# Encoder layer, the hand-over from the convolutions to the tail: two gate jobs make their own first products, net outputs rotate over seven rooms, five units of fillers stand in one fixed order

## The chip, the core and the metric

One core of a Trainium2 chip runs the whole layer as one program. The metric is the device time of one launch in microseconds (us), the median of several runs. The engines that matter here are TensorE (PE, matrix products, with PEld for its weight loads), VectorE (DVE), ScalarE (ACT), GpSimd (POOL) and SyncE, whose queue (SP) issues most DMA transfers. Each engine works through its own list of instructions in order; semaphores hold an instruction back until what it needs is there.

## The reference, cut to what matters

Two batches of 1024 rows by 1024 channels go through the same layer (`y_prompt` and `y_sample`, here b = 0 and b = 1):

```python
p = rmsnorm(x, g_pre) @ w_in
fv, fg, hv, hg, mg = split(p)          # widths 1024, 1024, 3072, 1024, 2048
fz  = fft over sequence and over 4 channel groups of fv, real part
y_f = (fz * silu(fg)) @ w_fourier_out
v, x1, x2 = split(short_conv(hv, w_short))
z = v
for n, gate in enumerate((x1, x2)):
    z = gate * long_conv(z, kf[:, n], hyena_d[n])      # by FFT of length 2L
y_h = (z * silu(hg)) @ w_hyena_out
g_f, g_h = split(sigmoid(mg + b_merge))
out = (g_f * y_f + g_h * y_h) @ w_out
y = x + rmsnorm(out, g_post)
```

## The kernel before, in words

Everything is float32. A product is made of three passes of TensorE: each operand is cut into a rounded high part and a rest (`split`: a cast on ACT, a subtraction on DVE or POOL), and high x high, high x low and low x high are added up in PSUM. Twelve matmuls of 128x512 (four blocks of the inner dimension, three passes) are the unit of work in what follows; `times` issues twelve.

Three phases follow one another: `phase_fourier`, `phase_main` (gates and convolutions) and `phase_tail`.

**The end of the main phase.** `branches` walks over 32 steps, 16 for each batch; a step is one long convolution of 128 channels (`conv_front`, `conv_back`). The last four steps also take units of *fillers* from the list `FIRST`, one, one, two and two; the units left over run after the last step. A unit (`spill_first`, L1062 to L1104) holds two gate jobs. A job is named (section, c): sections 5 and 6 are the two merge gates, 0 and 4 the SiLU gates of the two branches, and c is a group of 128 channels. For each job of a unit it makes twelve matmuls over the first half of the inner dimension (q = 0), then twelve over the second (q = 1), both into its half of one PSUM tile `pin`. Behind the q = 0 matmuls ACT copies the half sum into a tile `m` (L1091), and SP stores it in DRAM as `d_p` (L1092): the tail needs that half sum once more. Each batch of twelve matmuls wants a loaded weight `wr` (L1080, two rooms), cut into `wh` and `wl` (three rooms of each).

A unit called with `wide` true has more room: two more rooms for weights (`wx`), one tile of its own for both `m`, another for `fz`; and its first matmuls are put behind the last ones of the unit before it (`self.filler`), so that wide units run in one order, batch by batch. Units called with `wide` false are placed by the scheduler as it likes. Before, only the units of the last step and those behind it are wide: four of eight.

**The tail, its gates.** `phase_tail` makes the second half of batch 1's gates. Its 16 jobs (list `gates`) cover two groups of channels and two halves of the rows each, by Winograd's form of Strassen's scheme: seven products of twelve matmuls in place of eight. `PH` names them for the nets: 11, 12, s2, s1, s4, s3, 22. The first two products of each job were made in the main phase; `opened` (L1458) loads `m` = `d_p`, and ACT copies it into PSUM, where the next products are added. Each job so has five products left: s2 x T2, s4 of the job before x B22, s3 x T3, 22 of the job before x T4, s1 x T1. The left operands come from `prepare`, a generator that is advanced by hand between the products: load `wraw` (1 MB), then sums and splits s2, s3, s1, s4, 22. The right operands T1 to T4 lie in four `rooms` of 1 MB, loaded from `d_t` (`load_t`) and split in place (`round_t`). `gate_out` evacuates a result to a `gt` tile and stores it in `d_g`; in sections 0 and 4 it also loads `fz`, applies SiLU and multiplies.

**The tail, its nets.** Then come 4 x 28 products (`product(s)`, s = 0 to 111) for the two output projections of each branch and batch. `load_w` and `weight` bring and split their weights, `block` their right operands, and `step` places that work at fixed points between the products. Sixteen of each 28 products end in `net_out` (L1571): DVE subtracts or adds into a `gt` tile (three rooms), multiplies by the gate `g`, and the result goes to `d_m`: by SP in nets 0 and 2, and by POOL with an accumulating DMA (L1582) in nets 1 and 3. A room is free again once its transfer has landed. Eight `rows` of the last projection follow; `opening` prepares the first one of them while net 3 still runs, in the tiles s1h, s1l and sum among others.

The tile framework gives every engine its order by simulating the program; `tc.issue_after(i)` puts instructions of the same engine behind instruction `i`. A dependency between tiles counts the whole tile: the q = 0 matmuls of a unit's second job wait for the copy of the first job's half sum.

Of the kernel before, what the change touches and what calls it, by code (L numbers as in the profile page):

```python
# [16 lines left out]
P = 128  # L17
# [144 lines left out]
class K:  # L162
# [897 lines left out]
    def spill_first(self, jobs, ws, wide):  # L1060


        nc, a, wp = self.nc, self.a, self.wp
        ps = self.psum("mm", 2, "pin", L)
        at = lambda i: ps[:, 512 * i:512 * i + 512]
        last = self.filler if wide else None
        room = self.xp.tile([P, L], F32, tag="x13", name="m", bufs=1) if wide else None
        fz = self.xp.tile([P, L], F32, tag="x12", name="fz", bufs=1) if wide else None
        for q in range(2):
            for i, (sec, c) in enumerate(jobs):  # L1070
                k = self.taken % 5
                self.taken += wide
                if wide and k < 2:
                    t = self.xp.tile([P, 2, 512], F32R, tag=f"x1{k}", name="wx", bufs=1)
                    h, l = [t[:, j].rearrange("p (a b) -> p a b", a=4) for j in range(2)]
                else:
                    h, l = [wp.tile([P, 4, P], F32R, tag=t, name=t, bufs=3) for t in ("wh", "wl")]
                hf, lf = [t.rearrange("p a b -> p (a b)") for t in (h, l)]
                r = wp.tile([P, 512], F32, tag="w", name="wr", bufs=2)
                self.filled = nc.sync.dma_start(r, a["w_in"][sec, c][:, 512 * q:512 * q + 512])  # L1080
                self.split(hf, lf, r, "pool", "act")
                self.pooled = self.left
                with self.tc.issue_after(last.ins) if last else ExitStack():
                    for kk in range(4):
                        x = self.X[4 * q + kk][0]
                        for j, (w, d) in enumerate(((h, x[0]), (h, x[1]), (l, x[0]))):
                            done = self.mm(at(i), w[:, kk], d, q + kk + j == 0, kk + j == 5, True)
                last = done
                if q == 0:
                    m = room[:, 512 * i:512 * i + 512] if wide else wp.tile([P, 512], F32, tag="gt", name="m", bufs=3)  # L1090
                    nc.scalar.copy(m, at(i))  # L1091
                    nc.sync.dma_start(self.d_p[sec, c], m)  # L1092
        for i, (sec, c) in enumerate(jobs):
            t = wp.tile([P, 512], F32, tag="gt", name="gt", bufs=3)
            if sec in (0, 4):
                f = fz[:, 512 * i:512 * i + 512]
                nc.sync.dma_start(f, (self.d_sh if sec else self.d_fz)[1][c][:, 0:512])
                nc.scalar.activation(t, at(i), AF.Silu)
                self.mul("dve", t, t, f)
            else:  # L1100
                nc.scalar.copy(t, at(i))
            nc.sync.dma_start(self.d_g[1][sec][c][:, 0:512], t)
        self.filler = last
# [147 lines left out]
    def branches(self, nb, nct, ws, mi):  # L1251
# [49 lines left out]
        for i, (b, n, c) in enumerate(steps):  # L1301
            nxt = None
            if i + 1 < len(steps):
                nxt = front(i + 1)
                gates(i + 1)
                if i + 2 < len(steps) and steps[i + 2][0] != steps[i + 1][0]:
                    self.load_x(steps[i + 2][0])
            y = self.conv_back(n, c, B, ws)
            close(i + 1)
            B = nxt  # L1310
            for _ in range({4: 1, 3: 1, 2: 2, 1: 2}.get(len(steps) - i, 0)):
                self.spill_first(units.pop(0), ws, i + 1 == len(steps))
            z = self.gate(n, c, y, X.pop(i))
            if self.due:
                mark = mi.tile([P, 1], F32R, tag="mark", name="mark", bufs=1)
                with tc.issue_after(nc.gpsimd.tensor_copy(mark, z[:, 0:1]).ins):
                    self.due.pop(0)()
            if n == 0:
                Z[c] = z
                continue  # L1320
            nc.sync.dma_start(self.d_sh[b][c], z)
            if b == 0 and NF <= c:
                self.spill_gate(0, 0, c, ws)
# [17 lines left out]
        self.stt("dve", s[:, 1], s[:, 0], -1.0, r[:, 3], MUL, SUB)  # L1341
        self.add("dve", s[:, 3], s[:, 1], r[:, 2])

    FIRST = [((s, c), (s, c + 2)) for s in (5, 6) for c in (0, 4)] + [((0, c), (4, c)) for c in range(0, 8, 2)]

    def block_sums(self, r, u, k, rows):

# [36 lines left out]
    def phase_tail(self):  # L1384
# [2 lines left out]

        tc, nc, a = self.tc, self.nc, self.a
        wp, xp = self.wp, self.xp
        gates = [(s, c) for c in range(0, 8, 2) for s in (0, 4, 5, 6)]  # L1390
        rows = [(u, t) for u in range(4) for t in (0, 2)]
        nets = [("f", 0), ("h", 0), ("f", 1), ("h", 1)]
        flat = lambda t: t.rearrange("p a b -> p (a b)")
# [1 line left out]
        with ExitStack() as es:  # L1395
# [7 lines left out]
            def prepare(nm, s, c):  # L1403
# [16 lines left out]
                    A[n] = h, l  # L1420
                if opening:
                    parts("11", wp, ("w", "w"), r[:, 0], 2)
                elif nm == "o":
                    parts("11", wp, ("wh", "wl"), r[:, 0], 3)
                    parts("12", wp, ("wh", "wl"), r[:, 1], 3)
# [33 lines left out]
            def opened(job):  # L1459
                m = wp.tile([P, 512], F32, tag="wh", name="m1", bufs=3)  # L1460
                nc.sync.dma_start(m, self.d_p[job])
                p = self.psum("X", 2, "pg")
                if job in gates[:2]:
                    x = self.X[4][1][0]
                    self.mm(p, x[:, 0:P], x, True, True)
                nc.scalar.copy(p, m)
                return p

            def first(A, Y):
                pa, pb = self.psum("mm", 4, "pg"), self.psum("X", 2, "pg")  # L1470
                self.times(pa, A["11"], Y["B11"], True)
                m1 = kept(pa)
                self.times(pb, A["12"], Y["B21"], True)
                return pa, pb, m1
# [96 lines left out]
            def net_out(s, p, q, op2):  # L1571
                nm, b = nets[s // 28]
                c, m, o = out_of(s)
                t = wp.tile([P, 512], F32, tag="gt", name="gt", bufs=3)
                if q is not None:
                    self.tt("dve", t, p, q, op2)
                self.mul("dve", t, p if q is None else t, G[s])
                dst = self.d_m[2 * b + m][:, c]
                if nm == "f":
                    nc.sync.dma_start(dst, t)  # L1580
                else:
                    nc.gpsimd.dma_start(dst, t, accum_op=ADD)  # L1582
# [166 lines left out]
            rooms = [gs.tile([P, 2, 4, 512], F32R, tag=f"t{q}", name=f"room{q}", bufs=1) for q in range(4)]  # L1749
            act, dve, sp = self.rounded.ins.engine, self.left.ins.engine, self.filled.ins.engine  # L1750
            behind = lambda: tc.issue_after(newest(sp))
            prep = prepare("g", *gates[0])
            with tc.issue_after(self.filled.ins):
                next(prep)
            for j, q in order[:2]:
                with behind():
                    load_t(rooms[q], 0, int(j[1]) - 1)
            with behind():
                pa = opened(gates[0])
            j, q = order[2]  # L1760
            with behind():
                load_t(rooms[q], 0, int(j[1]) - 1)
            next(prep)
            Y = {"B22": [self.X[4 + k][1] for k in range(4)]}
            for j, q in order[:2]:
                for k in range(2):
                    round_t(rooms[q], k)
            pairs = lambda z: [(t[:, 0], t[:, 1]) for t in z]
            quad = lambda t: [(t[:, 0, k], t[:, 1, k]) for k in range(4)]
            for j, q in order:  # L1770
# [15 lines left out]
            A = list(next(prep) for _ in range(2))[-1]  # L1786
            for k in range(2):
                round_t(rooms[order[2][1]], k)
            past = None
            for i, job in enumerate(gates):  # L1790
                to = i + 1 - len(gates)
                more = prepare("g", *gates[i + 1]) if to else None
                ahead_of = (lambda: next(more)) if to else (lambda: None)

                def mark(n):
                    t = n - 5 + 5 * to
                    if t >= -6:
                        step(t)
                with ExitStack() if i else behind():
                    ahead_of()  # L1800
                if i == 0:
                    with behind():
                        load_t(rooms[order[3][1]], 0, 3)
                self.times(pa, A["s2"], Y["T2"], False)
                u = wp.tile([P, 512], F32, tag="wl", name="u", bufs=3)
                nc.scalar.copy(u, pa)
# [25 lines left out]
                B = ahead_of()  # L1832
                past = job, A, pa, pc, u
                if to:
                    A, pa, prep = B, opened(gates[i + 1]), more
                    if 2 <= i < 6:
                        r = [cell(xp, f"x1{2 * (i % 2) + j}", f"ws{j}") for j in range(2)]
                        with tc.issue_after(self.fetched.ins):
                            pinned(self.block_sums, [r[q // 2][:, q % 2] for q in range(4)], 1, i - 2,
                                   [a["w_out"][(i - 2 + 4 * j) * P:(i - 1 + 4 * j) * P] for j in range(2)])  # L1840
# [136 lines left out]
```

## Time and profile before

| what | us |
|---|---|
| median of the runs shown (2368.45 to 2373.16) | 2372.25 |
| the profiled execution, its own time | 2370.79 |
| its span in the trace | 2369.0 |
| PE busy | 2325.3 (98%) |
| DVE busy | 1985.3 (84%) |
| ACT busy | 1126.1 (48%) |
| POOL busy | 417.8 (18%) |
| mean granted TensorE clock | 0.995 |

The page counts a matmul from its start to its modelled end, and consecutive matmuls overlap: a busy PE is one without gaps, not one at its peak. In the traces below a start time is in us from the start of the span, then comes the duration; a bracket at the end of a timeline row says how long the engine had been idle and what ended that.

### The profile page before, as it was taken

How to read it: one execution, taken by the hardware profiler on the slowest of the kernel's cores; microseconds unless marked ns; L12 is line 12 of the kernel's file. 1: busy time of each engine (PE TensorE's matmuls, PEld its weight loads, DVE VectorE, ACT ScalarE, POOL GpSimd, SP SyncE). 2: the span in 40 equal slices, each digit the busy share in tenths (PEclk: the TensorE clock that was granted, in tenths of full speed). 3: DMA queues.
4: the chain of work that ended last, by engine and by line, in shares of the span. 5: the costliest groups of instructions: out<-in, count | busy, mean ns of one | idle time of the engine just before them, and what ended most of it. 6: DMA issues, size and time to landing. Idle time of an engine off the chain costs nothing.

```text
span 2369.0 us, 36468 instructions
## 1 busy us (share of the span) xinstructions
PE 2325.3 (98%) x12834; PEld 2019.9 (85%) x12834; DVE 1985.3 (84%) x3485; ACT 1126.1 (48%) x2111; POOL 417.8 (18%) x405
## 2 busy tenths in 40 slices
PE   8999999999999999999999999998999999999998
PEld 7998888888888888888888888886878888788787
DVE  8875788888889999999999989996766677786887
ACT  7645667666643333333322223333434465466443
POOL 1002212322432343330000001123000000101211
PEclk9999999999999999999999999999999999999999
DMA  8636855455766666667556555567875788989654
GB/s 281 231 106 227 274 188 173 154 176 175 231 224 211 197 218 205 213 179 249 172 176 177 173 163 163 185 198 249 285 257 188 254 296 265 245 281 272 169 160 142
DMA packets 255425, 496.50 MB, mean 210 GB/s; under 512 B 25606, under 2 KB 83304, under 8 KB 254922
## 3 DMA queue, kind: packets, MB, share of 16 engines
q1 hardware_dynamic: 231229, 419.03, 54.3%
q0 software_dynamic: 23792, 75.11, 11.3%
q8 instruction: 101, 1.65, 0.3%
q14 instruction: 82, 0.67, 0.1%
q10 hardware_dynamic: 221, 0.04, 0.0%
HBM read 339.41 MB, written 181.93 MB: 220 GB/s over the span
## 4 chain that ended last, share of the span: by engine, by line
PE 46%; issue 6%; DMA 4%; DVE 3%; POOL 1%; ACT 1%; SPq 0%; DVEq 0%; POOLq 0%; ACTq 0%
PE pin L195 17%; PE pg L195 12%; PE pn L195 6%; PE pT L195 5%; PE pX L195 5%; DMA room<-d_t 1%; PE tph L1115 1%; DMA d_m<-gt 1%; DMA ws<-in_w_out 1%; DMA wraw<-in_w_in 1%; DMA oB<-d_wo 0%; POOL d_m L1582 0%; DVE gt L182 0%; DMA wr<-in_w_in 0%; DVE ws L182 0%
## 5 line engine op out<-in xcount | busy, mean ns | idle before, releaser
L195 PE MATMUL pin<-x,wh 128*128 128x512 f32 x2760 | 872.3, 392 | 7.7 <-ACT m L1091 7.7
L195 PEld LDWEIGHTS pin<-x,wh 128*128 128x128 f32 x2760 | 513.4, 189 | 105.8 <-ACT m L1091 8.7
L195 PE MATMUL pin<-x,wl 128*128 128x512 f32 x1380 | 540.8, 392 | 0.0
L182 POOL TENSOR_TENSOR wl<-wr,wh 128x512 fp32r<-128x512 f32 x137 | 235.7, 1721 | 701.1 <-ACT wh L172 665.6
L195 PEld LDWEIGHTS pin<-x,wl 128*128 128x128 f32 x1380 | 260.1, 188 | 49.1
L195 PE MATMUL pn<-room,wh 128*128 128x512 f32 x864 | 268.2, 392 | 1.9 <-DVE gt L182 1.9
L195 PEld LDWEIGHTS pn<-room,wh 128*128 128x128 f32 x864 | 163.2, 189 | 37.3 <-DVE gt L182 2.8
L195 PE MATMUL pn<-room,wl 128*128 128x512 f32 x432 | 169.5, 392 | 4.2 <-DVE wl L182 4.2
L182 DVE TENSOR_TENSOR t<-pX,k 128x1024 f32<-128x1024 f32 x128 | 156.2, 1220 | 8.9 <-DMA k<-d_k 5.1
L195 PE MATMUL pX<-bh,cfwd 128*128 128x256 f32 x768 | 161.7, 289 | 0.6 <-DVE t L182 0.6
L172 ACT CAST wh<-wr 128x512 fp32r<-128x512 f32 x137 | 84.7, 618 | 130.1 <-PE pin L195 70.8
L195 PE MATMUL pT<-cinv,yh 128*128 128x256 f32 x768 | 145.3, 284 | 0.5 <-DVE T0s L182 0.5
L172 ACT CAST bh<-b 128x512 fp32r<-128x512 f32 x144 | 88.6, 619 | 94.2 <-DVE b L182 65.7
L195 PEld LDWEIGHTS pX<-bh,cfwd 128*128 128x128 f32 x768 | 126.4, 190 | 3.7 <-DVE t L182 1.5
L195 PEld LDWEIGHTS pT<-cinv,yh 128*128 128x128 f32 x768 | 122.6, 191 | 5.9 <-issue 0.6
L1582 POOL DMA_DIRECT2D d_m<-gt x32 | 27.3, 884 | 536.5 <-DVE gt L182 535.4
L172 ACT CAST yh<-y 128x512 fp32r<-128x512 f32 x96 | 59.4, 619 | 126.9 <-DVE y L182 126.8
L195 PE MATMUL pT<-cinv,yl 128*128 128x256 f32 x384 | 109.2, 284 | 0.5 <-DVE yl L182 0.4
L195 PE MATMUL pX<-bl,cfwd 128*128 128x256 f32 x384 | 109.3, 285 | 0.0
L182 DVE TENSOR_TENSOR bl<-b,bh 128x512 fp32r<-128x512 f32 x144 | 103.0, 719 | 5.0 <-ACT bh L172 4.9
L195 PEld LDWEIGHTS pn<-room,wl 128*128 128x128 f32 x432 | 81.8, 189 | 21.8 <-DVE wl L182 4.6
L182 DVE TENSOR_TENSOR y<-t 128x512 f32<-128x512 f32 x128 | 93.7, 732 | 3.0 <-PE pT L195 2.5
(383 smaller groups left out, 5124.5 us busy)
## 6 DMA issues: line engine op xcount, KB each, us to landing
k<-d_k SPq DMA_DIRECT2D x128, 512.0 KB, 4.3
wr<-in_w_in SPq DMA_DIRECT2D x144, 256.0 KB, 3.6
d_g<-gt SPq DMA_DIRECT2D x124, 256.0 KB, 2.9
wl<-d_s SPq DMA_DIRECT2D x56, 512.0 KB, 5.4
d_k<-kt SPq DMA_DIRECT2D x128, 128.0 KB, 2.3
d_k<-kt SPq DMA_DIRECT2D x64, 256.0 KB, 2.7
wraw<-in_w_in SPq DMA_DIRECT2D x32, 512.0 KB, 4.8
g<-d_g SPq DMA_DIRECT2D x64, 256.0 KB, 5.2
```

Source lines behind the costliest of these rows:

```text
L172: self.rounded = nc.scalar.copy(h, src)
L182: return e.tensor_tensor(out, a, b, op=op)
L195: return self.nc.tensor.matmul(out, lhsT, rhs, start=start, stop=stop, skip_group_check=shared)
L1115: nc.tensor.transpose(tp[:, q * P:(q + 1) * P], eo[:, e, q], self.ident)
L1582: nc.gpsimd.dma_start(dst, t, accum_op=ADD)
```

## The change

1. Jobs (5, 0) and (6, 0) (`OPEN`) leave the fillers: seven units of two jobs are left of eight, 14 half sums of 16. At the head of the tail, `prepare` also splits their operands 11 and 12, and `first` makes their two products (24 matmuls a job) into PSUM tiles of their own; the ACT casts for it are put behind the last copy of a half sum (`self.held`). They go in front of `gates`, whose order of sections becomes 5, 6, 0, 4 in place of 0, 4, 5, 6. Their first result leaves through `gate_out` right there.
2. The loads at the head of the tail are in this order, each behind the one before: `wraw` of the first job, `wraw` of the second, T2, T3, T1, T4. Before, it was `wraw` of the first, T2, T3, the half sum of the first, T1, then `wraw` of the second, T4.
3. The two matmuls in `opened` that only filled PSUM tiles of the first two jobs (into `pg`, from `x` alone) go.
4. The units of the last two steps are wide (`len(steps) - i < 3`), with those behind them five of seven.
5. Net outputs with s < 84 rotate over seven rooms (three `gt`, then the tiles u, s1h, s1l and sum, which the gates have left), those of net 3 over four (three `gt` and u).

```diff
@@ -1088,7 +1088,7 @@
                 last = done
                 if q == 0:
                     m = room[:, 512 * i:512 * i + 512] if wide else wp.tile([P, 512], F32, tag="gt", name="m", bufs=3)
-                    nc.scalar.copy(m, at(i))
+                    self.held = nc.scalar.copy(m, at(i))
                     nc.sync.dma_start(self.d_p[sec, c], m)
         for i, (sec, c) in enumerate(jobs):
             t = wp.tile([P, 512], F32, tag="gt", name="gt", bufs=3)
@@ -1309,7 +1309,7 @@
             close(i + 1)
             B = nxt
             for _ in range({4: 1, 3: 1, 2: 2, 1: 2}.get(len(steps) - i, 0)):
-                self.spill_first(units.pop(0), ws, i + 1 == len(steps))
+                self.spill_first(units.pop(0), ws, len(steps) - i < 3)
             z = self.gate(n, c, y, X.pop(i))
             if self.due:
                 mark = mi.tile([P, 1], F32R, tag="mark", name="mark", bufs=1)
@@ -1341,7 +1341,8 @@
         self.stt("dve", s[:, 1], s[:, 0], -1.0, r[:, 3], MUL, SUB)
         self.add("dve", s[:, 3], s[:, 1], r[:, 2])
 
-    FIRST = [((s, c), (s, c + 2)) for s in (5, 6) for c in (0, 4)] + [((0, c), (4, c)) for c in range(0, 8, 2)]
+    OPEN = [(5, 0), (6, 0)]
+    FIRST = [((5, 2), (5, 4)), ((6, 2), (6, 4)), ((5, 6), (6, 6))] + [((0, c), (4, c)) for c in range(0, 8, 2)]
 
     def block_sums(self, r, u, k, rows):
 
@@ -1387,7 +1388,7 @@
 
         tc, nc, a = self.tc, self.nc, self.a
         wp, xp = self.wp, self.xp
-        gates = [(s, c) for c in range(0, 8, 2) for s in (0, 4, 5, 6)]
+        gates = [(s, c) for c in range(0, 8, 2) for s in (5, 6, 0, 4)]
         rows = [(u, t) for u in range(4) for t in (0, 2)]
         nets = [("f", 0), ("h", 0), ("f", 1), ("h", 1)]
         flat = lambda t: t.rearrange("p a b -> p (a b)")
@@ -1420,6 +1421,15 @@
                     A[n] = h, l
                 if opening:
                     parts("11", wp, ("w", "w"), r[:, 0], 2)
+                elif nm == "g" and (s, c) in self.OPEN:
+                    for j in range(2):
+                        if (s, c) == self.OPEN[0]:
+                            t = cell(gw, f"st{j}", "wa", F32R)
+                            self.split(t[:, 0], t[:, 1], r[:, j], "dve", "act")
+                            A[("11", "12")[j]] = tri(t[:, 0]), tri(t[:, 1])
+                        else:
+                            parts(("11", "12")[j], wp, ("wh", "wl"), r[:, j], 3)
+                    yield A
                 elif nm == "o":
                     parts("11", wp, ("wh", "wl"), r[:, 0], 3)
                     parts("12", wp, ("wh", "wl"), r[:, 1], 3)
@@ -1460,14 +1470,11 @@
                 m = wp.tile([P, 512], F32, tag="wh", name="m1", bufs=3)
                 nc.sync.dma_start(m, self.d_p[job])
                 p = self.psum("X", 2, "pg")
-                if job in gates[:2]:
-                    x = self.X[4][1][0]
-                    self.mm(p, x[:, 0:P], x, True, True)
                 nc.scalar.copy(p, m)
                 return p
 
-            def first(A, Y):
-                pa, pb = self.psum("mm", 4, "pg"), self.psum("X", 2, "pg")
+            def first(A, Y, *where):
+                pa, pb = [self.psum(*w, "pg") for w in (where or (("mm", 4), ("X", 2)))]
                 self.times(pa, A["11"], Y["B11"], True)
                 m1 = kept(pa)
                 self.times(pb, A["12"], Y["B21"], True)
@@ -1571,7 +1578,11 @@
             def net_out(s, p, q, op2):
                 nm, b = nets[s // 28]
                 c, m, o = out_of(s)
-                t = wp.tile([P, 512], F32, tag="gt", name="gt", bufs=3)
+                k = o % 7 if s < 84 else o % 4
+                if k < 3:
+                    t = wp.tile([P, 512], F32, tag="gt", name="gt", bufs=3)
+                else:
+                    t = gw.tile([P, 512], F32, tag=("u", "s1h", "s1l", "sum")[k - 3], name="gt", bufs=1)
                 if q is not None:
                     self.tt("dve", t, p, q, op2)
                 self.mul("dve", t, p if q is None else t, G[s])
@@ -1749,22 +1760,30 @@
             rooms = [gs.tile([P, 2, 4, 512], F32R, tag=f"t{q}", name=f"room{q}", bufs=1) for q in range(4)]
             act, dve, sp = self.rounded.ins.engine, self.left.ins.engine, self.filled.ins.engine
             behind = lambda: tc.issue_after(newest(sp))
-            prep = prepare("g", *gates[0])
+            preps = [prepare("g", *job) for job in self.OPEN]
             with tc.issue_after(self.filled.ins):
-                next(prep)
-            for j, q in order[:2]:
+                next(preps[0])
+            with behind():
+                next(preps[1])
+            for j, q in order:
                 with behind():
                     load_t(rooms[q], 0, int(j[1]) - 1)
-            with behind():
-                pa = opened(gates[0])
-            j, q = order[2]
-            with behind():
-                load_t(rooms[q], 0, int(j[1]) - 1)
+            with tc.issue_after(self.held.ins):
+                As = [next(p) for p in preps]
+            Y = {"B11": [self.X[k][0] for k in range(4)], "B21": [self.X[4 + k][0] for k in range(4)],
+                 "B22": [self.X[4 + k][1] for k in range(4)]}
+            pas, outs = [], []
+            for A in As:
+                pa, pb, m1 = first(A, Y, ("X", 2), ("T", 2))
+                pas.append(pa)
+                outs.append((pb, m1))
+            prep = preps[0]
             next(prep)
-            Y = {"B22": [self.X[4 + k][1] for k in range(4)]}
             for j, q in order[:2]:
                 for k in range(2):
                     round_t(rooms[q], k)
+            for job, (pb, m1) in zip(self.OPEN, outs):
+                gate_out(job, 0, 0, pb, m1, ADD)
             pairs = lambda z: [(t[:, 0], t[:, 1]) for t in z]
             quad = lambda t: [(t[:, 0, k], t[:, 1, k]) for k in range(4)]
             for j, q in order:
@@ -1786,21 +1805,18 @@
             A = list(next(prep) for _ in range(2))[-1]
             for k in range(2):
                 round_t(rooms[order[2][1]], k)
-            past = None
+            past, pa = None, pas[0]
             for i, job in enumerate(gates):
                 to = i + 1 - len(gates)
-                more = prepare("g", *gates[i + 1]) if to else None
+                more = preps[1] if i == 0 else prepare("g", *gates[i + 1]) if to else None
                 ahead_of = (lambda: next(more)) if to else (lambda: None)
 
                 def mark(n):
                     t = n - 5 + 5 * to
                     if t >= -6:
                         step(t)
-                with ExitStack() if i else behind():
+                if i:
                     ahead_of()
-                if i == 0:
-                    with behind():
-                        load_t(rooms[order[3][1]], 0, 3)
                 self.times(pa, A["s2"], Y["T2"], False)
                 u = wp.tile([P, 512], F32, tag="wl", name="u", bufs=3)
                 nc.scalar.copy(u, pa)
@@ -1832,7 +1848,7 @@
                 B = ahead_of()
                 past = job, A, pa, pc, u
                 if to:
-                    A, pa, prep = B, opened(gates[i + 1]), more
+                    A, pa, prep = B, opened(gates[i + 1]) if i else pas[1], more
                     if 2 <= i < 6:
                         r = [cell(xp, f"x1{2 * (i % 2) + j}", f"ws{j}") for j in range(2)]
                         with tc.issue_after(self.fetched.ins):
```

## The prediction

> **What bounds the kernel now.** I read the page first: TensorE is busy nearly throughout. So I asked for the busy time by stage, from the last convolutions to the last projection (columns: stretch, its length, then busy us and instruction counts of PE, PEld, DVE, ACT, POOL, the granted clock, DMA share, GB/s).
>
> ```profile
> PE 2325.3 (98%) x12834; PEld 2019.9 (85%) x12834; DVE 1985.3 (84%) x3485; ACT 1126.1 (48%) x2111; POOL 417.8 (18%) x405
> ...
> 1640.00:1660.00 20.00, 13.00 (x52) 10.06 (x52) 10.47 (x14) 10.21 (x16) 3.22 (x3) 0.89 0.94 339
> 1660.00:1680.00 20.00, 20.00 (x84) 16.36 (x84) 14.68 (x20) 10.14 (x16) 0.00 (x0) 0.94 0.81 305
> 1860.00:1880.00 20.00, 20.00 (x90) 16.57 (x89) 12.36 (x19) 9.83 (x17) 0.00 (x0) 1.00 1.04 391
> 1880.00:1900.00 20.00, 20.00 (x89) 16.44 (x89) 16.18 (x17) 10.38 (x15) 0.00 (x0) 1.00 0.73 225
> ...
> 2050.00:2100.00 50.00, 45.85 (x191) 37.33 (x190) 36.41 (x40) 32.67 (x45) 1.07 (x2) 0.93 0.89 271
> 2200.00:2250.00 50.00, 46.54 (x192) 37.89 (x193) 45.76 (x72) 22.88 (x44) 10.66 (x9) 0.93 0.56 141
> ```
>
> An undisturbed stretch of the tail holds 90 matmuls in 20 us (1860 to 1880), so one takes 20/90 = 0.222 us. The 20 us from 1640 hold only 52, at a clock of 0.89; the 50 us from 2050 and from 2200 hold 191 and 192 where 225 fit. So the time to be won lies in three places, each with an idle PE and a lowered clock behind it. The lists of waits say for whom (us in total, times, longest):
>
> ```profile
> PE pin L195 <- ACT m L1091: 10.7, 6, 5.4
> ...
> DVE gt L182 <- DMA d_m<-gt: 18.5, 9, 5.0
> ```
>
> The first place is the end of the fillers. PE's timeline, then ACT's, then the chain of waits with its matmul counts:
>
> ```profile
> 1585.61 0.73 PE L195 MATMUL pin<-x,wh 128*128 128x512 f32 x2 [1.29 <-ACT m L1091]
> ...
> 1612.23 0.39 PE L195 MATMUL pg<-x 128*128 128x512 f32 x1
> ...
> 1630.28 3.01 PE L195 MATMUL pin<-x,wx 128*128 128x512 f32 x12 [0.68 <-ACT m L1091]
> ...
> 1639.74 0.73 PE L195 MATMUL pin<-x,wh 128*128 128x512 f32 x2 [1.01 <-ACT m L1091]
> ...
> 1644.40 5.75 PE L195 MATMUL pin<-x,wx 128*128 128x512 f32 x24 [1.63 <-ACT m L1091]
> 1649.99 0.62 PE L195 MATMUL pin<-x,wh 128*128 128x512 f32 x2
> ...
> 1658.24 1.22 PE L195 MATMUL pin<-x,wh 128*128 128x512 f32 x2 [5.37 <-ACT m L1091]
> ...
> 1643.77 0.58 ACT L1091 COPY m<-pin 128x512 f32<-128x512 f32 x1
> ...
> 1650.74 0.62 ACT L172 CAST a2h<-wraw 128x512 fp32r<-128x512 f32 x1 [2.02 <-DMA wraw<-in_w_in]
> ...
> 1652.76 1.04 ACT L172 CAST room<-room 128x1024 fp32r<-128x1024 f32 x1 [0.67 <-DMA room<-d_t]
> 1653.71 1.08 ACT L1098 ACTIVATE gt<-pin 128x512 f32<-128x512 f32 x2
> ...
> 1657.60 0.59 ACT L1091 COPY m<-pin 128x512 f32<-128x512 f32 x1
> ...
> 1644.70 8.03 DMA room<-d_t
> ...
> 1658.24 4.92 PE pin L195 x12
> ...
> 1674.07 13.62 PE pg L195 x60
> ```
>
> The matmuls from 1644.40 end unit 7, those from 1649.99 are the first twelve of unit 8, the last one, and its second twelve wait until 1658.24 for the copy `m` of its own half sum. That copy could have started at about 1652.7; it started at 1657.60. ACT's list put casts of the tail in front of it (a2h, a room, with others behind), which had waited for their transfers: the first room's took 8.03 us and landed at 1652.74. So the last unit stands behind work of the tail that isn't wanted yet. In the earlier wide units the same wait is 0.68, 1.01 and 1.63.
>
> The other two places are in the nets. DVE's and PE's timelines, and the chain at each:
>
> ```profile
> 2048.40 0.69 DVE L182 TENSOR_TENSOR gt<-gt,g 128x512 f32<-128x512 f32 x1
> 2054.10 0.69 DVE L182 TENSOR_TENSOR gt<-pn,ku 128x512 f32<-128x512 f32 x1 [5.01 <-DMA d_m<-gt]
> 2054.71 1.22 DVE L182 TENSOR_TENSOR wl<-wl,wh 128x1024 fp32r<-128x1024 f32 x1
> ...
> 2049.18 1.05 ACT L172 CAST wh<-wl 128x1024 fp32r<-128x1024 f32 x1
> ...
> 2055.98 0.79 PE L195 MATMUL pn<-room,wl 128*128 128x512 f32 x1 [4.15 <-DVE wl L182]
> ...
> 2046.45 7.56 DMA d_m<-gt
> ...
> 2055.98 6.14 PE pn L195 x14
> ```
>
> DVE stood 5.01 us for a `gt` room whose accumulating transfer took 7.56 us; the split `wl` of the next net's weight was queued behind it, though its cast was there at 2049.18 + 1.05. PE lost 4.15 us.
>
> ```profile
> 2206.99 0.69 DVE L182 TENSOR_TENSOR gt<-pn,ku 128x512 f32<-128x512 f32 x1 [1.65 <-DMA d_m<-gt]
> ...
> 2208.80 1.29 DVE L182 TENSOR_TENSOR wl<-wraw,wh 128x512 fp32r<-128x512 f32 x2
> ...
> 2199.87 0.73 PE L195 MATMUL pn<-room,wh 128*128 128x512 f32 x2 [0.94 <-DVE gt L182]
> ...
> 2209.54 0.79 PE L195 MATMUL pg<-oB,wl 128*128 128x512 f32 x1 [3.46 <-DVE wl L182]
> ...
> 2200.84 6.06 DMA d_m<-gt
> ...
> 2209.54 5.49 PE pg L195 x12
> ```
>
> At the end of net 3 a 1.65 us wait for a room stands in front of the `wl` of the first row of the projection, and PE waits 3.46 us. All these counts of waits come from semaphores; the gaps of PE are in its own rows.
>
> **The change, part by part.**
>
> *What a long gap costs beside itself.* Of the tail's matmuls 60 take 13.62 us in the chain, 0.227 each. After the 5.37 us gap twelve took 4.92 where 2.72 would do: 2.20 lost. After 4.15 us, fourteen took 6.14 instead of 3.18: 2.96. After 3.46 us, twelve took 5.49: 2.77. After 1.63 us nothing is lost (the 24 matmuls from 1644.40 take 5.6). So a gap is dear from somewhere between 1.63 and 3.46 us. [...]
>
> *The two jobs at the head of the tail.* They are moved, not dropped: 48 matmuls leave the fillers and 48 come back. The two filling matmuls (one is at 1612.23) go: 2 x 0.227 = 0.45. What is won is unit 8's waiting. That is 5.37 + 2.20 = 7.57. In `first` the second product goes to a PSUM tile of its own and waits for no copy, and the casts of 11 and 12 stand behind the last half sum's copy. With the 0.45 the upper end is 8.0. The lower end is 0: unit 7 is now the last, and its two copies can fall behind casts in the same way. Only 11 and 12 are pinned; a2h, s1h, s3h and the rooms' casts are not. I take that one room cast (1.04) comes in front of each of the two copies, 2.1 us, since the second `wraw` now delays the rooms: 8.0 - 2.1 = 5.9.
>
> *The loads.* The head loads two `wraw` and four rooms, 6 MB, behind the last weight `wr` of unit 7 instead of unit 8.
>
> ```profile
> 1627.66 0.33 SPq L1080 DMA_DIRECT2D wr<-in_w_in  x1
> ...
> 1643.17 0.45 SPq L1080 DMA_DIRECT2D wr<-in_w_in  x1
> 1643.67 0.99 SPq L1410 DMA_DIRECT2D wraw<-in_w_in  x2
> ```
>
> That is 1627.66 by the old trace in place of 1643.17. At the 305 GB/s of the 20 us from 1660 they take 20 us, to about 1649 if nothing else stands in the queue, while T2 is first wanted after 48 more matmuls, at about 1650 + 10.9 = 1661. Cover 12 us; were it gone, PE would stop at s2 x T2 for what is missing. The two half sums that are no longer loaded and two stores fewer on SP: nothing, as SP is not waited for there. Moved past them on SP are the first job's half sum load and nothing that PE needs. POOL's queue has no part in it.
>
> *The fixed order of units 3 and 4.* No work is added. Each unit has two copies to wait for. Lower end: four of them uncovered at about 1 us (0.68 and 1.01 above), -4. Upper end: the 1.29 us of the row at 1585.61 goes, in which a copy stood behind two evacuations. The convolution's products lie between them in both orders; I take 0, between the ends.
>
> *The order of the gates.* Jobs of 0 and 4 come last now, with up to four more DVE multiplications of 0.69 us each: 5.5 us more in the 26.7 us of two jobs. In the 40 us from 1860 DVE is busy 12.36 + 16.18 = 28.5, so 11 are free, which cover it: 0. With the cover gone a weight of net 0 would be late, as at 2055.98, for 7.
>
> *Seven rooms in nets 0 to 2.* The 5.01 us wait goes: a room comes back after seven outputs at 12 x 0.222 = 2.7 us, 18.7 us, against 7.56 for the transfer. Next is the cast, done at 2050.23; the split can then end before the 2051.8 at which PE stopped. So 4.15 + 2.96 = 7.1 is won. The four new rooms are idle then: the gates have left them, and the opening of the projection takes three of them only after s = 84. Ends: 0 (another DVE wait takes its place) and 7.1.
>
> *Four rooms in net 3.* A room comes back after four outputs, 10.7 us, against 2 x 0.69 of DVE and 6.06 of transfer. The 1.65 us go, the wait of 3.46 becomes 1.81, nearer to the 1.63 that cost no clock, so 2.77 go too; and the 0.94 at 2199.87, which waits for a `gt`. Together 5.4. Ends 0 and 0.94 + 3.46 + 2.77 = 7.2.
>
> The sum: 5.9 + 7.1 + 5.4 = 18.4. The profiled execution took 2370.79, which gives 2352.4. It lies 1.46 below the median of the runs shown, 2372.25, on which the forecast stands: 2353.9, said as 2354.
>
> **The rivals.**
>
> *The late copy moves to unit 7.* ACT works in order, so a cast put early by the framework holds back a copy that is ready. The rows of 1650.74 to 1657.60 speak for it, as the rooms are still loaded behind a last unit. Against it: the second `wraw` stands in front of them, about 1 MB or 3 us. Then the first term is 0.45 instead of 5.9: 2359. [...]
>
> *The rooms are not the bound of the nets.* The waits for rooms go, and weights, `g` or the next `wraw` are late at the same places. The chain at both places runs through the room's transfer, which speaks against it. Then only the head's 5.9 remains: 2366.
>
> *The change doesn't do what it says:* the copy moves to unit 7 and the nets stay as they are. 2372.
>
> *Slower: uncovered copies.* Five units in one order, ten copies. In units 3 and 4 the framework can no longer put a convolution's products where it likes; if a copy of `m` comes as late as at 1658.24, it costs 7.6 each time. It takes three such, 22.8, to overrule the 18.4; that gives 2377. Against it: units 5 to 7, ordered so before, show 1.63 at most.
>
> **How the numbers follow.** The forecast has 0.42. The late copy has 0.27, nets unmoved 0.13, nothing done 0.08, slower 0.07. The remaining 0.03 is more than forecast: all upper ends, 8.0 + 1.3 + 7.1 + 7.2 = 23.6, give 2348.6. A measurement of this kernel tells about 0.2%, 4.7 us, from no change: 2367.5 to 2377. Faster are the forecast, the first two rivals and the remainder, less some of 2366, which lies near the bound: 0.82. Same is 0.12, slower 0.06. The range reaches from 2348 to 2368, which leaves out the last two rivals and some spread. The forecast's own range is 2349 to 2359.
>
> **What would show it.** No wait of PE for a copy `m` above 2 us, and a clock of 1.00 throughout 1620 to 1680; the two lone matmuls into `pg` gone; 14 half sums stored and loaded. DVE's wait for `d_m` below 6 us in all, the gaps at the change from net 1 to net 2 and before the first row below 2 us, and over 215 matmuls in each of those 50 us. Wrong would it be with a 4 us gap of PE just before or at the first gate products, or with a split behind another transfer in the nets.

## The result, and the profile after

| kernel | median us | ratio to before, 95% interval |
|---|---|---|
| before, four runs beside it | 2370.79 | |
| after (2351.01 to 2355.01) | 2353.31 | 0.9926 [0.9908, 0.9943] |

The change makes the kernel 17.5 us faster; 18.4 were forecast. Every run below is given in the same way: its median, its ratio to before as measured beside it, and the 95% interval of that ratio. The page of after, then its busy time by stretches (columns as in the prediction):

```profile
span 2349.2 us, 36451 instructions
...
PE 2317.9 (99%) x12832; PEld 2017.1 (86%) x12832; DVE 1986.4 (85%) x3491; ACT 1123.5 (48%) x2107; POOL 420.0 (18%) x401
```

```profile
1640.00:1660.00 20.00, 18.35 (x73) 14.59 (x74) 13.93 (x21) 12.40 (x19) 0.00 (x0) 0.91 0.92 322
1660.00:1680.00 20.00, 20.00 (x90) 16.54 (x89) 13.52 (x19) 8.42 (x14) 0.00 (x0) 1.00 0.42 152
...
2050.00:2100.00 50.00, 50.00 (x223) 41.40 (x222) 39.15 (x44) 33.62 (x45) 0.00 (x0) 1.00 0.90 302
...
2200.00:2250.00 50.00, 49.84 (x220) 41.28 (x221) 46.12 (x82) 21.44 (x47) 9.15 (x6) 1.00 0.47 148
```

Two matmuls fewer are the lone ones. The stretches from 2050 (nets) and from 2200 (in after all of it rows, as the work has moved forward by some 16 us) now hold 223 and 220 matmuls in 50 us, where 191 and 192 stood. The stretch from 1640 holds 73 instead of 52, but its clock is still 0.91. The waits of PE and DVE from 1480 to 2230 say what is left:

```profile
PE pin L195 <- ACT m L1091: 6.6, 5, 2.4
PE pg L195 <- ACT u L1466: 2.1, 1, 2.1
PE pn L195 <- DVE gt L182: 0.8, 1, 0.8
...
DVE gt L182 <- DMA d_m<-gt: 0.2, 1, 0.2
```

Where the 19.8 us between the two spans went is read from two rows in PE's timeline: the first product of the nets and the first of the last projection. Before, then after:

```profile
1882.53 0.61 PE L195 MATMUL pn<-n,wh 128*128 128x512 f32 x2
...
2202.74 2.88 PE L195 MATMUL pg<-oB,w 128*128 128x512 f32 x12
```

```profile
1875.73 0.62 PE L195 MATMUL pn<-n,wh 128*128 128x512 f32 x2
...
2186.91 2.88 PE L195 MATMUL pg<-oB,w 128*128 128x512 f32 x12
```

| stretch | before | after | difference | forecast |
|---|---|---|---|---|
| up to the nets (fillers, head, gates) | 1882.5 | 1875.7 | -6.8 | -5.9 |
| nets | 320.2 | 311.2 | -9.0 | -7.1 - 0.94 |
| rows to the end | 166.3 | 162.3 | -4.0 | -1.65 - 2.77 |

These are single executions. After was profiled a second time: its span is 2354.3, 5.1 us more, and its first product of the nets starts at 1880.71, 5.0 us later. By that run the first line would be -1.8. So the second and third lines carry more than the first.

### The profile page after: what moved, and what is told of

It is laid out like the page before. It is cut to its first block, busy times and chain, and to the rows that moved or that the text cites. A ratio compares the mean times of both kernels' runs of the same rounds, so it can differ in the third digit from the quotient of the medians.

```text
span 2349.2 us, 36451 instructions
## 1 busy us (share of the span) xinstructions
PE 2317.9 (99%) x12832; PEld 2017.1 (86%) x12832; DVE 1986.4 (85%) x3491; ACT 1123.5 (48%) x2107; POOL 420.0 (18%) x401
## 3 DMA queue, kind: packets, MB, share of 16 engines
q8 instruction: 101, 1.65, 0.3%
## 5 line engine op out<-in xcount | busy, mean ns | idle before, releaser
L195 PE MATMUL pin<-x,wh 128*128 128x512 f32 x2720 | 860.1, 392 | 5.3 <-ACT m L1091 5.3
L195 PEld LDWEIGHTS pin<-x,wh 128*128 128x128 f32 x2720 | 505.7, 188 | 103.0 <-ACT m L1091 7.5
L195 PE MATMUL pin<-x,wl 128*128 128x512 f32 x1360 | 533.1, 392 | 0.0
L182 DVE TENSOR_TENSOR wl<-wl,wh 128x1024 fp32r<-128x1024 f32 x56 | 68.3, 1222 | 33.2 <-ACT wh L172 32.2
L1116 ACT COPY xt<-tph 128x512 f32<-128x512 f32 x64 | 37.0, 588 | 123.4 <-PE tph L1115 123.3
```

The source lines that it names most:

```text
L182: return e.tensor_tensor(out, a, b, op=op)
L195: return self.nc.tensor.matmul(out, lhsT, rhs, start=start, stop=stop, skip_group_check=shared)
L1116: nc.scalar.copy(xt[:, e].rearrange("p a b -> p (a b)"), tp)
```

## The experiments

**The rooms alone.** Before, with the new `net_out`.

```diff
-                t = wp.tile([P, 512], F32, tag="gt", name="gt", bufs=3)
+                k = o % 7 if s < 84 else o % 4
+                if k < 3:
+                    t = wp.tile([P, 512], F32, tag="gt", name="gt", bufs=3)
+                else:
+                    t = gw.tile([P, 512], F32, tag=("u", "s1h", "s1l", "sum")[k - 3], name="gt", bufs=1)
```

> The kernel before with the change's rooms for net outputs alone (seven in nets 0 to 2, four in net 3). Theory, the sum of the prediction: the two gaps in the nets go and nothing else, 7.1 + 5.4 = 12.5 us faster; the span from the first net product to the first row of the projection shrinks by about 9 (as it did, 320.0 to 311.0), the rows by about 4; the 5.37 us gap in front of unit 8's second job stays. Rival, the nets' gaps only went because the head of the tail ended earlier and the transfers met otherwise: under 4 us faster, with a 4 us gap left at the change of nets.

Measured 2360.35, 0.9962 [0.9950, 0.9974], 9.6 us faster than before beside it. PE's two rows in its timeline:

```profile
1885.65 0.62 PE L195 MATMUL pn<-n,wh 128*128 128x512 f32 x2
...
2197.08 2.88 PE L195 MATMUL pg<-oB,w 128*128 128x512 f32 x12
```

The nets take 311.4, the rows 162.0 (span 2359.1), as in after. The 3.1 us lost ahead of the nets are scatter, as every engine has the same list as before up to there (after's two executions differ by 5.0 at that place). Both gaps were the rooms', and the rival "the rooms are not the bound" falls. The size is less sure: the stretches give 8.8 + 4.2 = 13.0, but the times 9.6, and 12.5 lies outside their interval, which ends at 11.9.

**The own first products alone.** After without the rooms and with the old `wide`; unit 4 keeps its separate `fz` tile.

```diff
-                self.spill_first(units.pop(0), ws, len(steps) - i < 3)
+                self.spill_first(units.pop(0), ws, i + 1 == len(steps))
...
-                k = o % 7 if s < 84 else o % 4
...
+                t = wp.tile([P, 512], F32, tag="gt", name="gt", bufs=3)
```

> The kernel before with the two jobs at the head of the tail alone (own first products, the casts behind the last half sum's copy, the order of loads and of gates); three rooms for net outputs, and only the units of the last step and behind it in a fixed order. (Unit 4, now one of SiLU jobs, gets the tile for fz.) Theory: 5.9 to 6.8 us faster, all of it ahead of the first net product; both gaps in the nets stay. Rival, the fixed order of units 3 and 4 makes the head's gain: under 2 us faster.

Measured 2362.44, 0.9973 [0.9965, 0.9982], -7.5. Its waits of PE and DVE keep the gaps of the nets and shorten the one of the last unit:

```profile
PE pin L195 <- ACT m L1091: 5.8, 5, 2.2
PE pg L195 <- DVE wl L182: 4.0, 1, 4.0
PE pn L195 <- DVE wl L182: 2.5, 1, 2.5
...
DVE gt L182 <- DMA d_m<-gt: 19.9, 9, 4.8
```

Not all of it lies ahead of the nets, as was expected: in the profiled execution 6.6 us do, and the gap at the change of nets is 2.48 in place of 4.15, though the rooms are as before. With the rooms' 9.6 the 7.5 make 17.1 of the 17.5 (by the ratios 9.0 + 6.4 = 15.4, where the two measurements of after give 17.5 and 15.2): two parts that add up, with little left for the fixed order.

**The fixed order alone, and the change without it.** Before with the one line, and after with the old one (and unit 4's `fz`).

```diff
-                self.spill_first(units.pop(0), ws, i + 1 == len(steps))
+                self.spill_first(units.pop(0), ws, len(steps) - i < 3)
```

> The kernel before with the units of the last two steps in a fixed order, and nothing else. Theory: no difference, within 2 us either way, with the 5.37 us gap still in front of the last unit's second job. Rival, the fixed order makes the head's gain: 5 to 7 us faster. Second rival, its copies are uncovered: 4 us slower.

> The changed kernel with only the units of the last step and behind it in a fixed order, as before (unit 4 gets the tile for fz). Theory: the time of the changed kernel within 2 us, 17 us faster than before. Rival, the fixed order makes the head's gain: 11 us faster than before only.

Alone it gave 2364.46, 0.9985 [0.9976, 0.9994]: between 3.6 us (by the ratio) and 5.5 us (by the medians) faster. Its twelve times lie in two groups, 2362 to 2364.5 and 2368 to 2369.7. Left out of the change it cost nothing that can be told: 2354.85, 0.9936 [0.9924, 0.9948]; after, measured once more with no edit, gave 2353.30, 0.9936 [0.9924, 0.9949]. With the order alone, the last unit's wait is 3.67 us in PE's timeline, where before had 5.37:

```profile
1654.50 4.29 PE L195 MATMUL pin<-x,wx 128*128 128x512 f32 x12 [3.67 <-ACT m L1091]
```

So it shortens the wait that the own products also shorten, and the two don't add up. In ACT's list of that run two room casts (at 1649.96 and 1652.91) stand in front of the copy, where before had three (1652.76, 1655.18 and 1656.65). Why the framework's list came out so, the runs don't say.

> The changed kernel once more, as a measure for the three beside it. Both theories: 2353, within 2 us.

**The casts out of the way.** In after the copy is late because of ACT's list (timeline of ACT, after):

```profile
1635.75 0.62 ACT L172 CAST a2h<-wraw 128x512 fp32r<-128x512 f32 x1 [5.74 <-DMA wraw<-in_w_in]
...
1638.84 0.62 ACT L172 CAST s3h<-wraw 128x512 fp32r<-128x512 f32 x1 [1.43 <-DVE wraw L182]
1639.36 1.08 ACT L1098 ACTIVATE gt<-pin 128x512 f32<-128x512 f32 x2
1640.33 0.59 ACT L1091 COPY m<-pin 128x512 f32<-128x512 f32 x1
```

ACT stood 5.74 us before `a2h`, a cast of the tail for the first of the two jobs, because the `wraw` for it hadn't landed; the evacuations and the copy queued behind. This run puts every ACT instruction of the head and the first gate job behind the last copy:

```diff
-            with tc.issue_after(self.held.ins):
-                As = [next(p) for p in preps]
+            pin = ExitStack()
+            pin.enter_context(tc.issue_after(self.held.ins))
+            As = [next(p) for p in preps]
...
+                if i == 0:
+                    pin.close()
```

> The changed kernel with every ACT cast of the first gate job's preparation and of the rooms put behind the last half sum's copy, not only those of 11 and 12. Theory, a cast that waits for its transfer (a2h in front of the copy, 5.74 us of idle ACT before it) holds the copy back by 1.9 us and the gap of 2.44 also costs clock: the gap in front of unit 7's second job falls to the 1.0 to 1.2 of the units before it, the slow matmuls behind it (1.3 to 1.7 us) go, about 3 us faster than the changed kernel. Rival, the copy is bound by the evacuations in front of it and the pinned casts are then late for the gate products: no gain or a new gap at the first gate products.

Measured 2352.17, 0.9925 [0.9911, 0.9939], as after. The wait fell from 2.44 to 1.82 only, and that is within scatter: with the casts left as in after it was 2.27 in after measured again, 1.82 in the run with the turned rooms and 1.56 in the run with three rooms in net 3 (both below). But now the copy waits with no cast in front of it. ACT's timeline, then SP's, then PE's:

```profile
1637.41 1.09 ACT L1098 ACTIVATE gt<-pin 128x512 f32<-128x512 f32 x2 [2.28 <-PE pin L195]
...
1641.27 0.58 ACT L1091 COPY m<-pin 128x512 f32<-128x512 f32 x1 [2.78 <-DMA d_sh<-x]
...
1629.66 1.76 SPq L1411 DMA_DIRECT2D wraw<-in_w_in  x4
...
1632.23 0.39 SPq L1092 DMA_DIRECT2D d_p<-m  x1
...
1641.91 1.03 PE L195 MATMUL pin<-x,wh 128*128 128x512 f32 x2 [1.82 <-ACT m L1091]
```

ACT is free at 1638.5, and the copy waits 2.78 us for a transfer. I read it as the store of unit 6's half sum: all wide units share one tile `m`, and that store was issued at 1632.23, behind both `wraw` (1629.66). (The trace names a transfer of another tile, `d_sh`, that ended then.) In the run with the own products alone the chain in front of the same copy names the store itself, with 8.17 us up to its landing:

```profile
1630.95 8.17 DMA d_p<-m
```

**Casts out of the way and rooms for `m`.** The next run tests that reading: the last unit's half sums go to free `gt` tiles.

```diff
+                    m = room[...] if wide and jobs is not self.FIRST[-1] else wp.tile([P, 512], F32, tag="gt", name="m", bufs=3)
```

> The changed kernel with the head's casts behind the last half sum's copy, and the last unit's half sums in gt rooms in place of the one tile that all wide units share. Theory, with the casts out of the way the copy still waited (2.78 us) for the shared tile, whose store of unit 6 was issued behind the two wraw and landed some 9 us later: now the gap in front of unit 7's second job is 1.0 to 1.2, as in the units before it, and the slow matmuls behind it go; 2 to 3 us faster than the changed kernel. Rival, the copy waits for the evacuations of unit 6 on ACT: the gap stays near 1.8.

Measured 2350.50, 0.9927 [0.9915, 0.9940]. In ACT's timeline the copy stands right behind its matmuls:

```profile
1637.61 1.09 ACT L1098 ACTIVATE gt<-pin 128x512 f32<-128x512 f32 x2 [2.28 <-PE pin L195]
...
1640.33 0.58 ACT L1091 COPY m<-pin 128x512 f32<-128x512 f32 x1 [1.63 <-PE pin L195]
```

No wait for `m` in the last unit is above 0.68 now, and no clock is lost there (1.00 from 1640 to 1660, where after had 0.91). So the tile that a late store held is shown as a cause. That the early casts add to it, ACT's list in after suggests, and the next run. The price of both is too small for the times: the ratio is after's.

**Without the hold.** After with nothing put behind the last copy.

```diff
-            with tc.issue_after(self.held.ins):
-                As = [next(p) for p in preps]
+            As = [next(p) for p in preps]
```

> The changed kernel with the casts of the two jobs' operands 11 and 12 not put behind the last half sum's copy. Theory, two casts more (1.15 us) stand in front of unit 7's first copy and wait for the same wraw, one more in front of the second: 1 to 2 us slower than the changed kernel. Rival, the store of the shared tile binds the copy anyway: no difference.

Measured 2355.66, 0.9951 [0.9938, 0.9965]. The wait of unit 7's second job is the longest of all runs with the own products, and the chain in front of it runs through the casts. PE's timeline:

```profile
1641.92 0.74 PE L195 MATMUL pin<-x,wh 128*128 128x512 f32 x2 [3.39 <-ACT m L1091]
```

Yet no clock is lost behind it: its twelve matmuls end 3.0 us later, and the granted clock of the 20 us from 1640 was 1.00. The interval meets those of after's 0.9926 and 0.9936. After wasn't measured beside this run; by the ratio to 0.9936 the hold is worth some 3.6 us, if anything.

**One PSUM tile for each job of a unit.** With that, a unit's second job doesn't wait for the copy of the first.

```diff
-        ps = self.psum("mm", 2, "pin", L)
-        at = lambda i: ps[:, 512 * i:512 * i + 512]
+        ps = [self.psum("mm", 2, "pin", L) for _ in range(2)] if wide else [self.psum("mm", 2, "pin", L)] * 2
+        at = lambda i: ps[i][:, 512 * i:512 * i + 512]
```

> The changed kernel with two PSUM tiles for each wide unit, one for each job, in place of one for both. Theory, the second job's first matmuls wait for the first job's copy only because a dependency counts the whole tile: the waits for the copy m (6.6 us in five) fall below 1.5 us in all and the slow matmuls behind the longest go, 5 to 7 us faster than the changed kernel. Rival, a unit then waits for both tiles of the unit before it to be evacuated, and for its weights: the waits come back at the units' heads, less than 2 us faster.

Measured 2347.74 (2343.37 to 2349.58), 0.9906 [0.9893, 0.9920], 5.6 us below after measured beside it, and the intervals of the two ratios (the other is [0.9924, 0.9949]) don't meet. PE's waits for the fillers from 1620 on:

```profile
PE pin L195 <- ACT gt L1098: 1.4, 1, 1.4
...
PE pin L195 <- ACT m L1091: 0.3, 1, 0.3
```

The 1.4 stand where the 2.44 stood, in front of unit 7's second job: it now waits for the evacuation of the unit before, as the rival said, but once only. Around 1600 PE waits 3.2 us in three pieces for DVE in the convolutions, which after doesn't. So these rows account for less than the 5.6 us.

**Net 3 with three rooms.** After with one number changed.

```diff
-                k = o % 7 if s < 84 else o % 4
+                k = o % 7 if s < 84 else o % 3
```

> The changed kernel with three rooms in net 3 and seven in the other nets, which separates the two terms of the rooms. Theory, the sum of the prediction: net 3's fourth room is worth 5.4 us less the gap of 2.1 at the first row's copy, so this is 3 us slower than the changed kernel, with the gap of 3.5 to 4 us ahead of the first row's split back, and no gap at the change from net 1 to net 2. Rival, the seven rooms alone took DVE's lag away and net 3 needs no fourth: no difference.

Measured 2358.09, 0.9959 [0.9945, 0.9973], by the ratio 5.4 us slower than after's 0.9936, with the old gap back in PE's timeline and in DVE's waits:

```profile
2199.45 0.80 PE L195 MATMUL pg<-oB,wl 128*128 128x512 f32 x1 [4.21 <-DVE wl L182]
...
DVE gt L182 <- DMA d_m<-gt: 7.0, 3, 3.1
```

The rows take 166.7, as before the change (166.3), and there is no gap at the change from net 1 to net 2. The one room more in net 3 carries that whole line of the table.

**The gap that came instead.** In after PE waits 2.08 us for the copy `u` in the first row. The chain at that place, then the timelines of PE and ACT:

```profile
2194.26 4.30 DMA d_m<-gt
...
2200.16 0.73 PE L195 MATMUL pg<-room,s1h 128*128 128x512 f32 x2 [2.08 <-ACT u L1466]
...
2198.39 0.63 ACT L1718 ACTIVATE sq<-o 128x512 f32<-128x512 f32 x1 [1.04 <-DVE o L182]
2199.02 0.60 ACT L172 CAST s2h<-wraw 128x512 fp32r<-128x512 f32 x1
2199.53 0.58 ACT L1466 COPY u<-pg 128x512 f32<-128x512 f32 x1
```

The chain says that the tile `u`, now a room of the nets, came back late. The first run turns the order of the four rooms in net 3, so that `u` is free earlier; the second puts the copy `u` ahead of `sq`, which waits for DVE, and adds the two tiles and the pinned casts.

```diff
# the first
-                k = o % 7 if s < 84 else o % 4
+                k = o % 7 if s < 84 else 3 - o % 4
# the second, first row only, with the edits of the casts and of the two tiles
-                out(job, 0, 0, pb, m1, ADD)
...
                 u = kept(pa, True)
+                with tc.issue_after(self.copied.ins):
+                    out(job, 0, 0, pb, m1, ADD)
```

> The changed kernel with the four rooms of net 3 in turned order, so that the tile u takes the outputs 0, 4, 8, 12 and not 3, 7, 11, 15. Theory, the room u was still in a transfer of the net's last output when the first row of the projection wanted it for its own copy, and TensorE stood 2.1 us for it: that gap goes, 1.5 to 2.1 us faster than the changed kernel, nothing else moves. Rival, the copy is late because of the casts in front of it on ACT: the gap stays.

> The changed kernel with two PSUM tiles for each wide unit, with the head's casts behind the last half sum's copy, and with the first row's copy u put ahead of its sum of squares on ACT. Theory: the 5.6 us of the two tiles stay; the 1.7 to 2.1 us gap at the first row goes, as the copy there stood behind a sum of squares that waited for DVE; together 2345.5, about 8 us faster than the changed kernel. Rival, another wait takes the gap's place at the first row: 2347.5.

The first: 2351.62, 0.9927 [0.9915, 0.9939], and the gap is 1.73, where after measured again has 1.75: not the room. Its ACT timeline shows `sq` and the copy as in after, one behind the other:

```profile
2198.99 0.63 ACT L1718 ACTIVATE sq<-o 128x512 f32<-128x512 f32 x1 [1.67 <-DVE o L182]
...
2200.12 0.57 ACT L1466 COPY u<-pg 128x512 f32<-128x512 f32 x1
```

The second: 2346.22 (2342.55 to 2348.76), 0.9908 [0.9894, 0.9921], the fastest median, 21.1 us below before and not to be told from the two tiles alone. Its waits of PE at that place:

```profile
PE pg L195 <- DVE wl L182: 1.2, 1, 1.2
...
PE pg L195 <- ACT u L1466: 0.8, 1, 0.8
```

The wait for `u` fell to 0.8. It is 1.74 with the two tiles alone and 1.73 with the pinned casts alone, so ACT's order was its cause. The rows take 162.4, against 163.1 with the two tiles alone: too little for the times to show. The wait for the split `wl` stands ahead of `u` in the same row and was 0.9 with the two tiles alone.

## Why the prediction came out

*The head, 5.9 forecast, 6.8 measured, and alone 7.5 (6.4 by the ratio).* The mechanism was right: the 5.37 us of the last unit behind casts of the tail are gone. A smaller wait stands in unit 7, where 2.1 us were allowed for two room casts; it came for other reasons. No room cast stood in front of a copy, but `a2h`, held by the `wraw` of its own job, with `s1h` and `s3h`, and beside them the store of unit 6's half sum, whose tile the copy wanted. The step that failed is the sentence on the loads, "nothing that PE needs" is moved past on SP: `d_p` was, and a copy waited for its tile. The tell-tales "no wait above 2 us" and "1.00 throughout" were wrong with it (2.44 and 0.91). So the rival of the late copy happened, in small: 2.44 us and 1.74 more, as twelve matmuls took 4.46 where 2.72 would do, against the 5.37 + 2.20 of before. With the 0.45 of the lone matmuls these rows make 3.8, and 5.0 with all waits for `m` counted (10.7 before, 6.6 after). Scatter of the stretch ahead of the nets (5.0 above) is larger than what is missing, so that the total came within 1 us of the forecast is luck in part. The reading that the copy of before "could have started at about 1652.7" isn't shown either: the last store of its shared tile was issued at 1647.10 only, behind three loads of rooms, in SP's timeline of before:

```profile
1644.70 1.89 SPq L1639 DMA_DIRECT2D room<-d_t  x3
1647.10 0.32 SPq L1092 DMA_DIRECT2D d_p<-m  x1
```

When that store landed, the trace doesn't say.

*The fixed order, 0.* Right on top of the other parts, wrong alone: a gain of 3.6 us by the ratio or 5.5 by the medians lies above the upper end of 1.3. The step left out, as far as ACT's list shows, is that a fixed order also changes ACT's list in front of the last unit's copy. The rival of uncovered copies fell; the waits of the units that it newly orders are 1.34 at most.

*The nets, 8.0 forecast, 9.0 measured, 8.8 alone; the rows, 4.4 forecast, 4.0 measured, 4.2 alone.* Right by their own steps: DVE's wait for rooms is 0.2. The step "the wait of 3.46 becomes 1.81" was not: it went altogether in the first profile of after (0.62 is left in the second), and 2.08 for `u` stands in its place, a wait that wasn't named. That the third line came out at 4.0 all the same is two errors that cancel.

*The gates' order, 0.* The stretch where the last gates end and the nets begin holds 89 matmuls in after as in before, at full clock:

```profile
1880.00:1900.00 20.00, 20.00 (x89) 16.44 (x89) 15.86 (x17) 15.27 (x21) 0.00 (x0) 1.00 0.86 274
```

*The clock.* The price of 2.2 to 3.0 us behind a long gap is no fixed one: twelve matmuls took 4.29 behind 3.67 us (the fixed order alone), 1.6 more than 2.72, where the 5.49 behind 3.46 us in before are 2.8 more. Nor does the length of a gap alone decide it here, as in the reading "dear from somewhere between 1.63 and 3.46 us": the chain shows twelve matmuls at 4.63 us behind a gap of 1.82 with the casts pinned, and at 3.05 behind the same 1.82 in the run with the turned rooms; the granted clock of the 20 us from 1640 was 0.91 in the first and 1.00 in the second. The two rows:

```profile
1641.91 4.63 PE pin L195 x12
```

```profile
1641.19 3.05 PE pin L195 x12
```

## What to carry to other kernels

Count the time until a buffer comes round against the whole trip of its transfer, and ask what is queued behind the instruction that waits: one room more took 4 us off a stretch whose wait for the room was only 1.65 us. Before moving work to the head of a phase, look on every engine and queue for the last work of the phase before: here a store queued behind early loads held a buffer that the last copy wanted (2.78 us of wait with the casts pinned), and early casts stood in front of that copy (the first of them behind 5.74 us of idle ACT in after). When a chain names a transfer, turn the order of the buffers once: here the gap stayed (1.73 against 1.75 us), and it was the engine's own list (0.8 with the copy put first).

## What was not expected of the hardware

In these runs a gap of PE has no sharp price. Gaps of 1.82 (casts pinned), 2.27 (after measured again) and 2.44 us (after) cost 1.5 to 1.9 us in the next twelve matmuls, which took 4.63, 4.23 and 4.46 us where 2.72 would do; the granted clock of the 20 us from 1640 was 0.91 in all three. Gaps of 1.34 and 2.08 us in after, 1.82 with the turned rooms and even 3.39 without the hold cost 0.1 to 0.3, at a granted clock of 1.00. What tells the two apart, no run here shows.
